# Five post- and pre-norms of a decoder layer: the sum of squares by one product with ones on all partitions, root and Newton step on full rows instead of a diagonal spread

## The chip, the cores and the metric

The kernel runs on one core of one Trainium2 chip. The metric is the device time of one execution in microseconds (us), as the median of three runs. The engines are named as in the profile: PE (TensorE, the matmul array), PEld (its weight loads), DVE (VectorE), ACT (ScalarE), POOL (GpSimd) and SP (which issues most transfers).

## The reference

One layer of a hybrid decoder trunk runs for a prompt of 512 tokens and for 32 sample tokens (8 sequences of 4). All is float32. Cut to what matters here:

```python
def _rmsnorm(x, g):
    x32 = x.astype(jnp.float32)
    y = x32 * lax.rsqrt(jnp.mean(x32 * x32, axis=-1, keepdims=True) + EPS) * g
    return y

def _layer(x, ...):
    m, ... = _mixer(_rmsnorm(x, norm_mix_pre), ...)      # projections, LRU branch, attention branch, w_out
    x = x + _rmsnorm(m, norm_mix_post)
    f, ... = _conv_ffn(_rmsnorm(x, norm_ffn_pre), ...)   # w_up (1024 x 8192), conv, gelu gate, w_down (4096 x 1024)
    x = x + _rmsnorm(f, norm_ffn_post)
```

`x` is 544 tokens by 1024 features. A norm needs, for every token, the sum of squares over 1024 features, the reciprocal root r of its mean, and the product of each feature with r and the feature's gain. The change touches the last three norms of the layer (`norm_mix_post`, `norm_ffn_pre`, and a part of `norm_ffn_post`), not the first.

## The kernel before, in words

Activations lie feature-major: a tile has 128 features on the partitions and tokens along the columns, so 1024 features are eight tiles. The 544 tokens are cut into two halves. Around the norms they are columns 0 to 272 and 272 to 544 (`HALF2`, 272 columns each); in the down projection they are 0 to 256 and 256 to 544 (`HALF`, so the second has 288). Every product is made in three parts: weights and activations are split into a high part (ACT) and the rest, the low part (DVE), and PE multiplies high by high, high by low and low by high.

**A norm, with features on the partitions.** ACT squares each of the eight tiles, DVE adds the squares up in one accumulator (`acc`, `accx`). The sum over the 128 partitions that remains is made by PE in `stats` (L1029): each block of 128 tokens of the accumulator is the stationary operand against one column of ones, so that the sums come out with tokens on the partitions, one column for each block (`pst`, 128 x 3 in PSUM). The last block has only 16 tokens of its own and is padded with zeros by a POOL memset. `newton_rstd` (L389) then makes r on these three columns: a square root on ACT, a scale, a reciprocal and a Newton step on DVE. As the tokens must come back along the columns, `diag` (L1041) scales the identity by r, block by block (`dg`), and `spread` (L1048) multiplies ones by that diagonal: `rep`, 128 x 272 in PSUM, holds r of each token on all partitions. Eight scalar_tensor_tensor instructions on DVE then take tile times gain times `rep`.

**Order of the work.** PE runs strictly as the code is written (manual schedule). Through the product with `w_out` ("out", L1229 copies its results into `mt`) ACT and DVE are ordered by the scheduler, which puts instructions written under `high_priority` ahead by 150 places; from `order_` on, behind the "out" product, ACT and DVE too run as the code is written. Work beside the main loop is written as generators: `start_at` registers one, and each `tick` (half a step of "out", or one slot of about twelve matmuls later) advances those whose time has come. A `yield 0.5` therefore means one slot later, `yield 1.0` two slots.

**Where the norms stand.** `norm_chain(a, acc)` (L1112) holds two norms for half a: `m` (`norm_mix_post`: sum, then `mt` times gain times r, x added by POOL or DVE, squares of the new x into `accx`) and `f` (`norm_ffn_pre`: sum, then `x1` times gain times r into `h2f` or `h2t`, then its high and low parts `b11`, `b21` for the first half, `b12`, `b22` for the second, which the first up products read). In each: `stats` in one slot, `diag` in the next (`YS`), `spread` and the use in the one after (`YA`, `YB`). The chain of half 0 runs while PE makes "out" for half 1; the chain of half 1 runs while PE makes the early up products (`pq`, L1396) of half 0, four pairs of column blocks by two halves of the features, sixteen units of twelve matmuls. In each slot `consumed` splits the weights of a unit four slots ahead (`wh_e` on ACT, `wl_e` on DVE). Behind the sixteen units PE transposes some state rows (`psf`) and then begins the same products for half 1.

At the end, `finish_b` (L1654) does the last norm for the second half's 288 columns: its sum is `stats` over `acc` and over `sq7` (the squares of the last tile, kept apart), then `diag`; two slots later come `spread` and the eight `ft` products with POOL additions. Between them stand held-back down products for half 0, whose results DVE adds into `ft`; then PE transposes `ft` (`turned`, tile `pfo`) and makes the last two blocks of 128 tokens with tokens on the partitions (`tokens`, `ends`), whose own norm (`ssq`, `rstd`) the change does not touch.

All working tiles of 128 x 572 come from one pool of ten (`T`, `T_BUFS`).

Of the kernel before, what the change touches and what calls it, by code (L numbers as in the profile page):

```python
# [14 lines left out]
ALU = mybir.AluOpType  # L15
AX = mybir.AxisListType

P = 128
# [105 lines left out]
def hawk_step(ctx, tc, I, O):  # L124
# [21 lines left out]
    def T(name, dt=F32):  # L146
        return tp.tile([P, FLAT + 4], dt, tag="t", name=name)
# [10 lines left out]
    def SM(name, shape, tag="sm"):  # L158
        return smp.tile(shape, F32, tag=tag, name=name)
# [4 lines left out]
    def mm(out, l, r, start, stop):  # L164
        pe.matmul(out, l, r, start=start, stop=stop)  # L165
# [223 lines left out]
    def newton_rstd(r, v, s_, sq):  # L389

        act.activation(s_, sq, AF.Sqrt, scale=1.0 / D, bias=epst)
        dve.tensor_scalar(v, sq, 1.0 / D, EPS, ALU.mult, ALU.add)
        dve.reciprocal(r, s_)
        mul(s_, r, r)
        stt(s_, s_, -0.5, v, ALU.mult, ALU.mult)
        stt(r, s_, 1.5, r, ALU.add, ALU.mult)
# [629 lines left out]
    mixer.close()  # L1026


    def stats(acc, nch, nm, more=None):  # L1029

        ps = PX("pst_" + nm)
        for z in range(nch):
            mm(ps[:, z:z + 1], acc[:, z * P:(z + 1) * P], ones[:, 0:1], z == 0, more is None and z == nch - 1)
        for z in range(nch if more is not None else 0):
            mm(ps[:, z:z + 1], more[:, z * P:(z + 1) * P], ones[:, 0:1], False, z == nch - 1)
        st = SM("nst_" + nm, [P, 3, 4], "nst")
        v, r, s_ = (st[:, z, :nch] for z in range(3))
        newton_rstd(r, v, s_, ps[:, :nch])
        return r

    def diag(r, n, nm):  # L1041
        dg = T("dg_" + nm)
        for z in range((n + P - 1) // P):
            w = min(P, n - z * P)
            dve.tensor_scalar(dg[:, z * P:z * P + w], ident[:, :w], r[:, z:z + 1], None, ALU.mult)
        return dg

    def spread(dg, n, nm):  # L1048

        rep = PX("rep_" + nm)  # L1050
        mm(rep[:, :n], ones, dg[:, :n], True, True)
        return rep

    def sq_sum(acc, src, n, first, nm):
        if first:
            act.activation(acc[:, :n], src, AF.Square)
            if n % P:
                pool.memset(acc[:, n:n + P - n % P], 0.0)
        else:
            sq = T("sq_" + nm)  # L1060
            act.activation(sq[:, :n], src, AF.Square)
            add(acc[:, :n], acc[:, :n], sq[:, :n])
# [49 lines left out]
    def norm_chain(a, acc):  # L1112
        lo, hi = HALF2[a]
        n = hi - lo
        nch = (n + P - 1) // P
        with tc.high_priority(offset=HP):
            r = stats(acc, nch, f"m{a}")
            yield YS[a]
            dg = diag(r, n, f"m{a}")
        yield YA[a]  # L1120
        with tc.high_priority(offset=HP):
            rep = spread(dg, n, f"m{a}")
            acc2 = T(f"accx{a}")
            sq = {}

            def x1_(c):
                return x1[c][:, lo:hi]

            for c in range(0 if a else 8):
                m_ = mt[c][:, lo:hi]  # L1130
                stt(m_, m_, pv[:, G_POST + c:G_POST + c + 1], rep[:, :n], ALU.mult, ALU.mult)
                pool.tensor_tensor(out=x1_(c), in0=x1_(c), in1=m_, op=ALU.add)
                sq_sum(acc2, x1_(c), n, c == 0, f"x{a}_{c}")
            for g in range(6 if a else 0):
                for c in range(2 * g, 2 * g + 2) if g < 4 else ():
                    m_ = mt[c][:, lo:hi]
                    stt(m_, m_, pv[:, G_POST + c:G_POST + c + 1], rep[:, :n], ALU.mult, ALU.mult)
                    if c % 2 == 0:
                        pool.tensor_tensor(out=x1_(c), in0=x1_(c), in1=m_, op=ALU.add)
                if g < 4:  # L1140
                    add(x1_(c), x1_(c), m_)
                for c in range(2 * g - 3, 2 * g - 1) if 1 <= g < 6 else ():
                    if 0 <= c < 8:
                        sq[c] = acc2 if c == 0 else T(f"sq_x{a}_{c}")
                        act.activation(sq[c][:, :n], x1_(c), AF.Square)
                        if c == 0 and n % P:
                            pool.memset(acc2[:, n:n + P - n % P], 0.0)
                for c in range(2 * g - 5, 2 * g - 3) if g < 5 else range(5, 8):
                    if c > 0:
                        add(acc2[:, :n], acc2[:, :n], sq[c][:, :n])  # L1150
                yield 0.5
        yield NORM_TICKS[a]
        with tc.high_priority(offset=HP):
            r = stats(acc2, nch, f"f{a}")
            yield YS[a]
            dg = diag(r, n, f"f{a}")
        yield YB[a]
        with tc.high_priority(offset=HP):
            rep = spread(dg, n, f"f{a}")

            def normed(c, dst):
                stt(dst, x1[c][:, lo:hi], pv[:, G_FPRE + c:G_FPRE + c + 1], rep[:, :n], ALU.mult, ALU.mult)

            def first(k2):
                return h2f[k2][:, 0:2 * HN]

            if a == 0:
                for k2 in range(5):
                    if k2 < 4:
                        for c in (2 * k2, 2 * k2 + 1):  # L1170
                            normed(c, h2_half0(c))
                        act.activation(operand2(("b11", "b21")[k2 // 2], k2 % 2, 0), first(k2), AF.Copy)
                    if k2:
                        o = [operand2(("b11", "b21")[(k2 - 1) // 2], (k2 - 1) % 2, j) for j in range(2)]
                        sub(o[1], first(k2 - 1), f32(o[0]))
                return
            n2 = {}

            def second(k2):
                return n2[k2]  # L1180

            def high(nm, src):
                for k in range(2):
                    act.activation(operand2(nm, k, 0), src(k), AF.Copy)

            def low(nm, src):
                for k in range(2):
                    sub(operand2(nm, k, 1), src(k), f32(operand2(nm, k, 0)))

            for k2 in range(5):  # L1190
                if k2 < 4:
                    n2[k2] = npool.tile([P, 2 * HN], F32, name=f"h2t{k2}")
                    for z in range(2):
                        normed(2 * k2 + z, n2[k2][:, z * HN:(z + 1) * HN])
                    act.activation(operand2(("b12", "b22")[k2 // 2], k2 % 2, 0), n2[k2], AF.Copy)
                if k2:
                    o = [operand2(("b12", "b22")[(k2 - 1) // 2], (k2 - 1) % 2, j) for j in range(2)]
                    sub(o[1], n2[k2 - 1], f32(o[0]))
                if k2 in (2, 4):
                    yield 0.5  # L1200
            for c in range(8):
                nc.sync.dma_start(out=x1d[c], in_=x1[c][:, 0:NT])
            t2 = [T(f"t2_{k}")[:, 0:2 * HN] for k in range(2)]
            for k in range(2):
                sub(first(k), first(k), second(k))
                stt(t2[k], first(k), -1.0, second(2 + k), ALU.mult, ALU.subtract)
                yield 0.5
            for k in range(2):
                add(first(2 + k), first(2 + k), t2[k])
                yield 0.5  # L1210
            high("t2", lambda k: t2[k])
            yield 0.5
            low("t2", lambda k: t2[k])
            yield 0.5
            for k in range(2):
                sub(second(k), second(k), second(2 + k))
                yield 0.5
            yield TX
            for nm, src in (("t3", second), ("t1", first), ("t4", lambda k: first(2 + k))):
                high(nm, src)  # L1220
                yield TY
                low(nm, src)
                yield TY
# [428 lines left out]
    sq7 = {}  # L1652

    def finish_b(acc):  # L1654

        lo, hi = HALF[1]
        n = hi - lo
        dg = diag(stats(acc, 3, "o1", sq7), n, "o1")
        yield FB[0]
        rep = spread(dg, n, "o1")  # L1660
        for c in range(8):
            f_ = ft[c][:, lo:hi]
            stt(f_, f_, pv[:, G_FPOST + c:G_FPOST + c + 1], rep[:, :n], ALU.mult, ALU.mult)
            pool.tensor_tensor(out=f_, in0=f_, in1=x1r[c][:, lo:hi], op=ALU.add)
            if c % 2:
                yield 0.5
# [178 lines left out]
```

## Time and profile before

| | us |
|---|---|
| median of three runs | 1009.07 (1008.91 to 1009.62) |
| the profiled execution, its own time | 1010.02 |
| its span, first to last instruction | 1008.1 |
| PE busy, with 7835 matmuls | 995.6 (99%) |
| DVE busy, 1553 instructions | 731.6 (73%) |
| ACT busy, 1422 instructions | 579.8 (58%) |
| POOL busy, 270 instructions | 151.5 (15%) |
| granted TensorE clock, mean | 0.995 |

By the chain of work that ended last and by the timeline, the first half's norms lie between 423 and 447 us, the second half's between 448 and 475, and the last norm between 982 and 992.

A row of the timeline reads: start, length, engine, line, operation, output <- inputs, shapes, count, and in brackets the idle time of the engine before it with what ended it. A group reads: line, engine, operation, count, then busy time and mean ns of one, then idle time and its releaser. A program sees float32 products of PE as two entries each, which is why three products show as x6.

### The profile page before, as it was taken

The page shows a single profiled execution, that of the slowest core. Times are in us where ns is not written, and L with a number is a line of the kernel's source. Part 1 is how long each engine was busy: PE and PEld are TensorE (multiplying, and loading weights), DVE is VectorE, ACT ScalarE, POOL GpSimd, SP SyncE. Part 2 cuts the span into 40 slices and gives each one's busy share as a digit, 9 for nine tenths or more (in the row PEclk, how much of TensorE's full clock was granted, in tenths as well). Part 3 has the DMA queues.
Part 4 walks back from the last instruction along what each step waited for, and adds up shares of the span by engine and source line. Part 5 has one row for each costly group of instructions (what it writes and reads, how often), then busy time and mean ns, then how long its engine had stood idle before and what let it go on. Part 6 is the DMA issues. An engine that isn't in the chain of part 4 may idle for free.

```text
span 1008.1 us, 20186 instructions
## 1 busy us (share of the span) xinstructions
PE 995.6 (99%) x7835; PEld 985.3 (98%) x7835; DVE 731.6 (73%) x1553; ACT 579.8 (58%) x1422; POOL 151.5 (15%) x270
## 2 busy tenths in 40 slices
PE   8999999999999999999999999999999999999997
PEld 7999999999999999999999999999999999999996
DVE  6476688444945655489787687878888888887865
ACT  6444554458448634556776656565656565656662
POOL 3131010001403432020000111111111111110004
PEclk9999999989999999999999999999999999999999
DMA  7743222322323245317235858585858676767712
GB/s 210 229 149 92 63 85 86 105 85 68 111 74 105 86 138 144 109 44 239 79 91 137 181 136 179 137 189 130 191 126 191 126 189 135 179 147 178 215 45 89
DMA packets 207687, 133.40 MB, mean 132 GB/s; under 512 B 6546, under 2 KB 194306, under 8 KB 207560
## 3 DMA queue, kind: packets, MB, share of 16 engines
q1 hardware_dynamic: 197944, 112.20, 39.2%
q0 software_dynamic: 9600, 17.90, 11.3%
q10 hardware_dynamic: 48, 2.03, 0.5%
q8 instruction: 61, 1.00, 0.4%
q14 instruction: 34, 0.28, 0.1%
HBM read 111.82 MB, written 9.14 MB: 120 GB/s over the span
## 4 chain that ended last, share of the span: by engine, by line
PE 93%; DVE 3%; DMA 2%; ACT 2%; issue 0%; SPq 0%; ACTq 0%; DVEq 0%
PE pmin L165 22%; PE pmdn L165 17%; PE pux L1396 15%; PE puy L1396 7%; PE pq L1396 6%; PE pmout L165 5%; PE pmao L165 5%; PE pmlo L165 4%; PE puz L1396 4%; PE pg L165 1%; PE psc L165 1%; PE pvp L165 1%; DMA raw_up_s<-in_w_up_dram 1%; DMA raw_in<-in_w_in_dram 1%; PE pt L701 1%; PE ptok L165 1%
## 5 line engine op out<-in xcount | busy, mean ns | idle before, releaser
L165 PE MATMUL pmin<-hH,wh_in 128*128 128x256 f32 (+1 forms) x576 | 168.0, 294 | 0.0
L165 PE MATMUL pmin<-hH,wl_in 128*128 128x256 f32 (+1 forms) x576 | 165.6, 290 | 0.0
L165 PE MATMUL pmin<-hL,wh_in 128*128 128x256 f32 (+1 forms) x576 | 165.5, 289 | 0.0
L165 PE MATMUL pmdn<-fH,wh_dn 128*128 128x256 f32 (+1 forms) x448 | 129.2, 288 | 0.2 <-DVE ft L174 0.2
L165 PE MATMUL pmdn<-fH,wl_dn 128*128 128x256 f32 (+1 forms) x448 | 129.2, 288 | 0.2 <-DVE wl_dn L168 0.2
L165 PE MATMUL pmdn<-fL,wh_dn 128*128 128x256 f32 (+1 forms) x448 | 129.1, 288 | 0.0
L177 DVE SCALAR_TENSOR_TENSOR uc<-u,fv,uc 128x560 f32<-128x560 f32 x128 | 102.0, 797 | 13.3 <-ACT uc L1427 13.2
L165 PEld LDWEIGHTS pmin<-hH,wh_in 128*128 128x128 f32 x576 | 109.2, 190 | 1.7 <-issue 0.6
L165 PEld LDWEIGHTS pmin<-hL,wh_in 128*128 128x128 f32 x576 | 109.2, 191 | 0.0
L165 PEld LDWEIGHTS pmin<-hH,wl_in 128*128 128x128 f32 x576 | 108.8, 190 | 0.0
L165 PEld LDWEIGHTS pmdn<-fH,wh_dn 128*128 128x128 f32 x448 | 84.3, 188 | 0.6 <-issue 0.6
L165 PEld LDWEIGHTS pmdn<-fH,wl_dn 128*128 128x128 f32 x448 | 84.4, 188 | 0.4 <-DVE wl_dn L168 0.4
L165 PEld LDWEIGHTS pmdn<-fL,wh_dn 128*128 128x128 f32 x448 | 84.3, 188 | 0.0
L1522 ACT COPY u<-pux 128x272 f32<-128x272 f32 x52 | 20.1, 386 | 85.4 <-PE pux L1396 85.3
L168 DVE TENSOR_TENSOR u<-puy,u 128x240 f32<-128x240 f32 (+2 forms) x78 | 24.6, 344 | 49.8 <-PE puy L1396 32.5
L174 DVE TENSOR_TENSOR ft<-ft,pmdn 128x256 f32<-128x256 f32 (+1 forms) x104 | 45.2, 435 | 16.6 <-PE pmdn L165 16.0
L277 ACT ACTIVATE wh_in<-raw_in 128x512 fp32r<-128x512 f32 x72 | 44.2, 628 | 20.8 <-PE pmin L165 10.4
L282 DVE TENSOR_TENSOR wl_in<-raw_in,wh_in 128x512 fp32r<-128x512 f32 x72 | 48.2, 683 | 1.6 <-ACT wh_in L277 1.5
L1427 ACT ACTIVATE uc<-u,fv 128x560 f32<-128x560 f32 x64 | 48.2, 755 | 0.0
L664 ACT ACTIVATE s<-s,st 128x256 f32<-128x256 f32 (+1 forms) x32 | 15.2, 476 | 50.7 <-DVE st L661 43.3
L168 DVE TENSOR_TENSOR wl_dn<-raw_dn,wh_dn 128x512 fp32r<-128x512 f32 x56 | 38.3, 685 | 0.0
L1322 POOL DMA_DIRECT2D raw_up_s<-raw_up_s x26 | 22.7, 872 | 101.7 <-issue 5.2
(773 smaller groups left out, 3415.7 us busy)
## 6 DMA issues: line engine op xcount, KB each, us to landing
raw_in<-in_w_in_dram SPq DMA_DIRECT2D x36, 512.0 KB
raw_dn<-in_w_down_dram SPq DMA_DIRECT2D x56, 256.0 KB
raw_up_s<-in_w_up_dram SPq DMA_DIRECT2D x26, 512.0 KB
raw_up_s<-raw_up_s POOLq DMA_DIRECT2D x26, 256.0 KB, 6.1
raw_ao<-in_w_attn_o_dram SPq DMA_DIRECT2D x8, 512.0 KB
raw_lo<-in_w_lru_o_dram SPq DMA_DIRECT2D x8, 512.0 KB
raw_out<-in_w_out_dram SPq DMA_DIRECT2D x8, 512.0 KB
x1d<-x SPq DMA_DIRECT2D x8, 272.0 KB
```

Of the source, the lines that this page charges most:

```text
L165: pe.matmul(out, l, r, start=start, stop=stop)
L168: dve.tensor_tensor(out=out, in0=a, in1=b, op=ALU.subtract)
L174: dve.tensor_tensor(out=out, in0=a, in1=b, op=ALU.add)
L177: dve.scalar_tensor_tensor(out=out, in0=a, scalar=s_, in1=b, op0=op0, op1=op1)
L277: act.activation(hl[0], raw, AF.Copy)
L282: (eng or dve).tensor_tensor(out=hl[1], in0=raw, in1=f32(hl[0]), op=ALU.subtract)
L664: act.activation(s3[:, j, :], s3[:, j, :], AF.Exp, bias=ng[:, j:j + 1], accum_out=sm[:, j:j + 1])
L701: pe.transpose(pt[:, (2 * ch + j) * P:(2 * ch + j + 1) * P], s3[:, j, ch * P:(ch + 1) * P], ident)
L1322: pool.dma_start(out=w["p4"], in_=w["p2"], accum_op=ALU.add)
L1396: pe.matmul(ps[:, :HN], w, x, start=start and k == 0 and i == 0, stop=stop and k == 3 and i == 2, skip_group_check=True)
L1427: act.activation(yt[j][:, 0:FLATU], u[:, 0:FLATU], AF.Copy, scale=fv[:, j:j + 1])
L1522: act.copy(e[nm_], z)
```

## The change

The sum over partitions is now one product with the whole 128 x 128 block of ones as the stationary operand and the accumulator as the moving one: every partition of the result holds the sum of every token, with tokens along the columns. Root and Newton step run on 128 x 272 (288 in the last norm) instead of 128 x 3, with the result and two working values in tiles of the pool `T`; the result stays in SBUF. `diag`, `spread` and the padding memsets are gone. Root and Newton step are written one `yield` later than before, where `diag` was (in `finish_b`: where `spread` was, two slots later).

```diff
-    def stats(acc, nch, nm, more=None):
+    def sums_(acc, n, nm, more=None):
 
         ps = PX("pst_" + nm)
-        for z in range(nch):
-            mm(ps[:, z:z + 1], acc[:, z * P:(z + 1) * P], ones[:, 0:1], z == 0, more is None and z == nch - 1)
-        for z in range(nch if more is not None else 0):
-            mm(ps[:, z:z + 1], more[:, z * P:(z + 1) * P], ones[:, 0:1], False, z == nch - 1)
-        st = SM("nst_" + nm, [P, 3, 4], "nst")
-        v, r, s_ = (st[:, z, :nch] for z in range(3))
-        newton_rstd(r, v, s_, ps[:, :nch])
+        mm(ps[:, :n], ones, acc[:, :n], True, more is None)
+        if more is not None:
+            mm(ps[:, :n], ones, more[:, :n], False, True)
+        return ps
+
+    def rstds(ps, n, nm):
+
+        r, v, s_ = (T(z + nm)[:, :n] for z in ("nr_", "nv_", "ns_"))
+        newton_rstd(r, v, s_, ps[:, :n])
         return r
-
-    def diag(r, n, nm):
-        dg = T("dg_" + nm)
-        for z in range((n + P - 1) // P):
-            w = min(P, n - z * P)
-            dve.tensor_scalar(dg[:, z * P:z * P + w], ident[:, :w], r[:, z:z + 1], None, ALU.mult)
-        return dg
-
-    def spread(dg, n, nm):
-
-        rep = PX("rep_" + nm)
-        mm(rep[:, :n], ones, dg[:, :n], True, True)
-        return rep
 
     def sq_sum(acc, src, n, first, nm):
         if first:
             act.activation(acc[:, :n], src, AF.Square)
-            if n % P:
-                pool.memset(acc[:, n:n + P - n % P], 0.0)
...
     def norm_chain(a, acc):
...
         with tc.high_priority(offset=HP):
-            r = stats(acc, nch, f"m{a}")
+            ps = sums_(acc, n, f"m{a}")
             yield YS[a]
-            dg = diag(r, n, f"m{a}")
+            rep = rstds(ps, n, f"m{a}")
         yield YA[a]
         with tc.high_priority(offset=HP):
-            rep = spread(dg, n, f"m{a}")
             acc2 = T(f"accx{a}")
...
                         act.activation(sq[c][:, :n], x1_(c), AF.Square)
-                        if c == 0 and n % P:
-                            pool.memset(acc2[:, n:n + P - n % P], 0.0)
...
         with tc.high_priority(offset=HP):
-            r = stats(acc2, nch, f"f{a}")
+            ps = sums_(acc2, n, f"f{a}")
             yield YS[a]
-            dg = diag(r, n, f"f{a}")
+            rep = rstds(ps, n, f"f{a}")
         yield YB[a]
         with tc.high_priority(offset=HP):
-            rep = spread(dg, n, f"f{a}")
...
     def finish_b(acc):
...
-        dg = diag(stats(acc, 3, "o1", sq7), n, "o1")
+        ps = sums_(acc, n, "o1", sq7)
         yield FB[0]
-        rep = spread(dg, n, "o1")
+        rep = rstds(ps, n, "o1")
```

More of the change, by code (lines that the diff above doesn't have):

```diff
@@ L1114, in norm_chain @@
         n = hi - lo
-        nch = (n + P - 1) // P
         with tc.high_priority(offset=HP):
-            r = stats(acc, nch, f"m{a}")
+            ps = sums_(acc, n, f"m{a}")
             yield YS[a]
-            dg = diag(r, n, f"m{a}")
+            rep = rstds(ps, n, f"m{a}")
         yield YA[a]
         with tc.high_priority(offset=HP):
-            rep = spread(dg, n, f"m{a}")
             acc2 = T(f"accx{a}")
```

## The prediction

> **What bounds the kernel now.** I read the page first (busy time, then the chain that ended last), then the same chain between 415 and 520 us where four of the five changed norms lie, then PE's waits there, then VectorE (DVE) in order of time.
>
> ```profile
> PE 995.6 (99%) x7835; PEld 985.3 (98%) x7835; DVE 731.6 (73%) x1553; ACT 579.8 (58%) x1422; POOL 151.5 (15%) x270
> PE 93%; DVE 3%; DMA 2%; ACT 2%; issue 0%; SPq 0%; ACTq 0%; DVEq 0%
> 447.00:475.00 28.00, 27.60 (x218) 27.04 (x217) 25.40 (x62) 15.09 (x35) 3.07 (x4) 1.00 0.62 194
> PE pst_f L165 <- DVE accx L174: 0.4, 1, 0.4
> ```
>
> TensorE (PE) is busy 99% of the span and carries 93% of the chain, at full granted clock (1.00 in the third row, whose columns are length, PE, weight loads, DVE, ACT, POOL, clock, DMA share, GB/s). So a microsecond of PE work removed is a microsecond won, if PE never has to wait longer than now. The third row is the warning: from 447 to 475 us, where the second half's two norms run, DVE is busy 25.4 of 28 us, and the one wait of PE in this stretch (fourth row) is for DVE's last addition into `accx`. There the kernel is a DVE chain with PE just behind it. That is where the change puts more DVE work.
>
> ```profile
> 423.23 0.56 PE pst_m L165 x6
> ...
> 437.87 0.56 PE pst_f L165 x6
> ...
> 446.53 1.51 PE pq L1396 x12
> 448.05 0.80 PE pst_m L165 x6
> ...
> 464.87 0.83 PE pst_f L165 x6
> ...
> 473.79 0.87 PE psf L1384 x8
> 474.66 42.16 PE pq L1396 x336
> ```
>
> These are pieces of the chain (start, length, what). A norm costs PE a `pst` (six entries for three one-column products) and later a `rep`, one product of 272 columns (two entries).
>
> **PE: work removed.** The new sum is one product of the shape of `rep`, and `rep` itself goes. So the saving per norm is the `pst`: 0.56 + 0.56 + 0.80 + 0.83 = 2.75 us in four norms. At the end of the kernel the `pst` has twice the entries:
>
> ```profile
> 982.33 1.23 PE pst_o L165 x12
> 986.53 0.48 PE rep_o L165 x2
> ```
>
> There 1.71 becomes two products of 0.48, 0.75 saved. Altogether 3.5 us of PE, if nothing stalls. The POOL memsets of the padding go too; nothing waits on POOL for them, so nothing for that.
>
> **DVE: work added.** Now the order on DVE round the second half's first norm:
>
> ```profile
> 447.82 1.35 DVE L168 TENSOR_TENSOR b21L<-h2f,b21H 128x544 fp32r<-128x544 f32 x2
> 449.18 0.16 DVE L392 TENSOR_SCALAR nst_m<-pst_m 128x3 f32<-128x3 f32 x1
> 449.26 0.17 DVE L393 RECIPROCAL nst_m<-nst_m 128x3 f32<-128x3 f32 x1
> 449.46 0.16 DVE L171 TENSOR_TENSOR nst_m<-nst_m 128x3 f32<-128x3 f32 x1
> 449.66 0.36 DVE L177 SCALAR_TENSOR_TENSOR nst_m<-nst_m 128x3 f32<-128x3 f32 x2
> 449.93 0.69 DVE L168 TENSOR_TENSOR wl_e<-raw_up__5740,wh_e 128x512 fp32r<-128x512 f32 x1
> 450.54 0.62 DVE L1045 TENSOR_SCALAR dg_m<-ident,nst_m 128x128 f32<-128x128 f32 x3
> 451.07 0.68 DVE L168 TENSOR_TENSOR wl_e<-raw_up__5738,wh_e 128x512 fp32r<-128x512 f32 x1
> 452.47 0.91 DVE L177 SCALAR_TENSOR_TENSOR mt<-mt,pv,rep_m 128x272 f32<-128x272 f32 x2 [0.71 <-PE rep_m L165]
> ```
>
> Newton on three columns takes 0.75 (449.18 to 449.93), the diagonal 0.53 (450.54 to 451.07): 1.28 in all. The prices on 272 columns:
>
> ```profile
> L509 DVE RECIPROCAL lz<-lz x1: 204/204/204, 59.4 to 59.4; 128x8 f32<-128x8 f32 x1
> L670 DVE RECIPROCAL st<-st 128x2 f32<-128x2 f32 x16 | 2.7, 166 | 0.6
> L177 DVE SCALAR_TENSOR_TENSOR mt<-mt,pv,rep_m 128x272 f32<-128x272 f32 x16 | 7.2, 488 | 1.4 <-PE rep_m L165 1.4
> L171 DVE TENSOR_TENSOR gl<-gl,pmlo 128x272 f32<-128x272 f32 x16 | 6.9, 431 | 1.3 <-PE pmlo L165 1.1
> 420.27 0.40 ACT L1229 ACTIVATE mt<-pmout 128x272 f32<-128x272 f32 x1 [2.14 <-PE pmout L165]
> ```
>
> A product or scale from PSUM takes 0.43, a scalar_tensor_tensor 0.49, and each step that needs the one before starts some 0.04 after its end (0.20 from start to start for 0.16 of work). The root on ACT goes from a few columns to the 0.40 of an activation of 272 columns.
>
> The term that decides is the reciprocal. Three columns take 0.17 us, eight take 0.204: 7.6 ns a column, where the other operations gain only some 1 ns a column (0.43 for 272 against 0.16 for 3). From eight to 272 columns that is 0.204 + 264 x 0.0076 = 2.2 us, far from any row, so it has two ends: 0.45 if the eight-column row is no slope at all and the reciprocal streams like the others, 2.2 by the slope. I take 2.2, because both rows are of this very operation. [...]
>
> The new Newton is then 0.35 (the scale overlaps the next) + 2.25 + 0.47 + 0.53 + 0.49 = 4.1 us on DVE in place of 1.28, in five norms, nearly all of it in the dependent chain.
>
> **First half (418 to 447 us).**
>
> ```profile
> 427.40 1.73 DVE L177 SCALAR_TENSOR_TENSOR mt<-mt,pv,rep_m 128x272 f32<-128x272 f32 x4 [0.73 <-PE rep_m L165]
> 427.98 6.92 POOL L1132 TENSOR_TENSOR x<-x,mt 128x272 f32<-128x272 f32 x8 [20.47 <-DVE mt L177]
> 430.85 0.61 DVE L174 TENSOR_TENSOR accx<-accx,sq_x 128x272 f32<-128x272 f32 x1
> 436.08 0.43 DVE L174 TENSOR_TENSOR accx<-accx,sq_x 128x272 f32<-128x272 f32 x1
> 442.14 1.72 DVE L177 SCALAR_TENSOR_TENSOR h2f<-x,pv,rep_f 128x272 f32<-128x272 f32 x4 [0.72 <-PE rep_f L165]
> 445.58 0.72 DVE L168 TENSOR_TENSOR b11L<-h2f,b11H 128x544 fp32r<-128x544 f32 x1
> ```
>
> Sum at 423.2, plus 0.5 product, 0.5 root, 4.1 of Newton, less the 0.35 that runs beside the root, with part of a weight split between: the eight `mt` products start near 428.4, 1.0 late. The old path waited 0.7 for `rep`, which is why it is not more. Beside POOL's additions a DVE addition of two SBUF tensors takes 0.61, alone 0.43, while the `mt` products, whose third operand is in PSUM, stay at 0.49. The new root lies in SBUF, so those products should get the same 0.1 to 0.2 each: 0.6 more over this loop. [...] `accx` is complete at 436.5 now, so 438.1; PE, 0.6 early by the first saving, reaches the second sum at 437.3 and waits 0.8. The second Newton runs from there to 443.0 against 442.14. The second `b11L` comes near 447.1, about when PE's first `pq` wants it (a quarter to a half of the way through the piece at 446.53). So PE enters the second half about where it does now: the savings of two norms are eaten by waits, and DVE is 1.0 late.
>
> **Second half (447 to 477 us).** ACT and DVE now take work as it is written, and PE consumes a unit of weights every 1.5 us. The Newton steps move one slot back, behind one `wl_e`; behind them are queued the next `wl_e`, the `mt` products and all that follows. So b21L ends at 450.2 instead of 449.2, `wl_e` 450.8, Newton 454.9, `wl_e` 455.5, and the `mt` products start at 455.5 against 452.47: 3.0 late. The loop after it is full DVE up to the sum at 464.87, so nothing is made up; contention adds 0.2. PE waits for `accx` (and a little for the late `wl_e`) some 4 to 5 us, having nothing else in its order.
>
> ```profile
> 466.54 0.15 DVE L392 TENSOR_SCALAR nst_f<-pst_f 128x3 f32<-128x3 f32 x1
> 469.39 1.72 DVE L177 SCALAR_TENSOR_TENSOR h2t<-x,pv,rep_f 128x272 f32<-128x272 f32 x4 [0.89 <-issue]
> 473.93 1.54 DVE L168 TENSOR_TENSOR b22L<-h2t,b22H 128x544 fp32r<-128x544 f32 x2
> ```
>
> The last norm: now 2.85 from Newton's start to the `h2t` products (0.89 of it idle); then one `wl_e` and 4.1, 4.7 in all: 1.8 more. DVE is 5.0 late at the last `b22L`, 480.5 instead of 475.5. PE reads it first after one `pq` of 1.5 and half of another behind 474.66, that is at 476.9: 1.4 of slack. So PE comes out 3.6 late. Behind it the chain is one PE piece of 42 us; nothing gives it back.
>
> **The end.**
>
> ```profile
> 985.31 0.74 DVE L174 TENSOR_TENSOR ft<-ft,pmdn 128x256 f32<-128x256 f32 x2
> 987.05 0.94 DVE L177 SCALAR_TENSOR_TENSOR ft<-ft,pv,rep_o 128x288 f32<-128x288 f32 x2 [1.00 <-PE rep_o L165]
> 987.91 0.41 DVE L174 TENSOR_TENSOR ft<-ft,pmdn 128x256 f32<-128x256 f32 x1
> 989.80 0.44 PE pfo L1696 x4
> ```
>
> `finish_b` now takes root and Newton only after its pause, where `rep` stood. They follow the two `ft` additions, which end near 985.3 since PE is a little earlier; 288 columns need 4.2 us, so the `ft` products start at 989.5 instead of 987.05, and the `ft` addition behind the first two (987.91) ends at 990.8. PE's `pfo` transposes need that one: they would come at 989.0, by 0.75 saved, and go at 990.9, 1.1 later than the 989.80 of now. ACT's copy of `pfo` stands behind a square that waits for DVE's `frow`, itself behind four more products: 2 us late. The rest of the end is a serial chain: 1.7 late, between 1.1 and 2.0.
>
> **Sum.** 3.6 + 1.7 = 5.3 us slower. The profiled execution took 1010.02 (span 1008.1 and 1.9 round it), which gives 1015.3; it stands 0.95 above the median of the runs, 1009.07, so on that scale 1014.4.
>
> **Rivals.** First, the reciprocal streams at 0.45 and the new chain is 2.3 us. Then each norm's result is ready at or before the old `rep` (0.7 to 0.9 of idle was spent waiting for it), DVE is 1.1 ahead in the second half, PE keeps 1.8 to 2 of its 2.75, and 0.4 at the end: 1006.8, faster. The point from which it decides is a Newton of about 2.9 us, a reciprocal of 1.0. For it: the eight-column row is one single instruction; against it: at two and three columns the same operation takes 0.17 in every row, so it does not scatter by 0.04.
>
> Second, the price is right but half of the lateness is swallowed: the first half absorbs its own, the split of weights runs ahead, and the end's ACT chain hides 1 us. Then some 1.5 + 0.5 of loss against the forecast's 5.3 would be left, at 1010.5. Against it: DVE has 0.7 and 0.9 of idle in the second half, and I have already spent both.
>
> Third, a place that I have not priced: three working tiles of 272 columns come from the ten shared temporaries, where one diagonal did. If a square or a `u` tile has to wait for one of them, a step of 4 us repeats once: 1018.5. For it: they are held through a reciprocal; against it: no wait of the page now names a temporary.
>
> **How the numbers follow.** Forecast 0.72, fast reciprocal 0.10, absorbed 0.08, temporaries 0.10. With the reciprocal between 1.9 (the slope from two to eight columns) and 2.2, contention nothing to 1 us and the end's two bounds, the forecast itself reaches from 1011.5 to 1017. The range is 1010.5 to 1019, which leaves out the first rival and a part of the others. A measurement of this kernel can tell 0.2%, 2.0 us, from no change: faster 0.09, same 0.09, slower 0.82.
>
> **What would show it.** Right: a RECIPROCAL of 272 columns near 2.2 us; PE idle before the sum near 465 of several us on `accx`, and a shorter one at the first products of the second half; DVE busy some 14 us more; PE's busy time about 3.5 less; `pfo` waiting on DVE. Wrong: a reciprocal under 1 us, or PE waits in 417 to 480 that add up to less than the 2.75 saved.

## The result, and the profile after

The changed kernel takes 1026.29 us (median of five runs, 1024.76 to 1027.73), the kernel before in the same runs 1008.91 (1005.94 to 1009.62): ratio 1.0177, 95% interval 1.0163 to 1.0191. So it is 17.4 us slower, where 5.3 were forecast and the range ended at 1019. The profiled execution is the one of 1024.76, span 1022.9.

The page of the kernel after, busy times and the engines' shares of the chain that ended last:

```profile
PE 993.8 (97%) x7801; PEld 981.8 (96%) x7801; DVE 748.4 (73%) x1538; ACT 580.7 (57%) x1422; POOL 152.0 (15%) x264
PE 84%; DVE 9%; ACT 3%; DMA 2%; issue 2%; SPq 0%; POOL 0%; ACTq 0%; DVEq 0%; POOLq 0%
```

The window of the second half's norms, with the columns explained in the prediction:

```profile
447.00:475.00 28.00, 23.89 (x167) 22.51 (x166) 26.71 (x51) 14.25 (x32) 3.59 (x4) 0.94 0.47 154
```

PE's waits from 400 us on (total us, times, longest), without the two shortest:

```profile
PE pst_f L165 <- DVE accx L174: 5.8, 2, 4.5
PE pux L1378 <- DVE wl_s_p L168: 2.8, 1, 2.8
PE pyo L1655 <- ACT yo L1657: 2.3, 1, 2.3
PE pq L1378 <- DVE b11L L168: 1.2, 2, 0.8
PE pfo L1678 <- DVE ft L174: 1.0, 1, 1.0
PE pq L1378 <- ACT b11H L1154: 1.0, 1, 1.0
PE pq L1378 <- DVE wl_q L168: 0.8, 1, 0.8
PE pq L1378 <- DVE wl_e L168: 0.7, 1, 0.7
PE pq L1378 <- DVE b22L L168: 0.4, 1, 0.4
```

Before, PE carried 93% of the chain and waited 0.4 us at one sum; now it carries 84%, and nine rows of waits stand there, 16 us together. The clock column of the window has fallen from 1.00 to 0.94, so PE lost speed too, not only time.

To see where the time went, take the starts of the same PE instructions in both traces, counted from the first sum (423.07 us before, 420.06 after). What lies ahead of that sum is the same work; the profiled run of before lost 2.9 us there to a drop of the granted clock between 200 and 224 us (0.86), which that of after did not have (1.00). All stages below are differences of such starts.

| stage | before | after | change |
|---|---|---|---|
| first sum to second (first half, `m` to `f`) | 14.64 | 18.59 | +3.95 |
| second to third (first half `f`, to the second half's `m`) | 10.34 | 14.48 | +4.14 |
| third to fourth (second half, `m` to `f`) | 16.82 | 19.01 | +2.19 |
| fourth to `psf` | 8.76 | 8.10 | -0.66 |
| `psf` to the last norm's sum | 508.53 | 513.54 | +5.01 |
| from there to the end of the span | 25.94 | 29.12 | +3.18 |

The sum is 17.81. The first half has lost 8.1, where the forecast had none; the second half 1.5 up to `psf`; the long stretch of up and down products behind it 5.0; the end 3.2. The 5.0 have two parts. Instruction by instruction, 1.8 of them are lost by 533 us: PE waits 0.43 for `b22L`, the last product of the second half's norm, and 0.78 for `wl_q`, a weight split of DVE, both in the list above. The other 3.2 are lost at one place, the wait of 2.77 for `wl_s_p` near 944 and the slow products behind it.

VectorE (DVE) in the first half of the kernel after, in order of time:

```profile
422.29 1.84 DVE L393 RECIPROCAL nr_m<-ns_m 128x272 f32<-128x272 f32 x1
424.05 0.63 DVE L168 TENSOR_TENSOR wl_e<-raw_up__5725,wh_e 128x512 fp32r<-128x512 f32 x1
424.59 0.43 DVE L171 TENSOR_TENSOR ns_m<-nr_m 128x272 f32<-128x272 f32 x1
424.94 0.69 DVE L168 TENSOR_TENSOR wl_e<-raw_up__5727,wh_e 128x512 fp32r<-128x512 f32 x1
...
427.20 3.69 DVE L177 SCALAR_TENSOR_TENSOR mt<-mt,pv,nr_m 128x272 f32<-128x272 f32 x5
430.82 1.02 DVE L174 TENSOR_TENSOR accx<-accx,sq_x 128x272 f32<-128x272 f32 x1
431.75 1.01 DVE L177 SCALAR_TENSOR_TENSOR mt<-mt,pv,nr_m 128x272 f32<-128x272 f32 x1
...
443.32 0.44 DVE L174 TENSOR_TENSOR acc<-acc,sq_wo 128x272 f32<-128x272 f32 x1 [4.37 <-ACT sq_wo L1048]
443.70 0.44 DVE L392 TENSOR_SCALAR nv_f<-pst_f 128x272 f32<-128x272 f32 x1
444.06 1.84 DVE L393 RECIPROCAL nr_f<-ns_f 128x272 f32<-128x272 f32 x1
```

POOL beside the `mt` products, and ACT ahead of the second Newton step, in the same view:

```profile
427.84 4.63 POOL L1117 TENSOR_TENSOR x<-x,mt 128x272 f32<-128x272 f32 x5 [32.04 <-DVE mt L177]
...
442.43 0.40 ACT L1211 ACTIVATE mt<-pmout 128x272 f32<-128x272 f32 x1 [4.30 <-PE pmout L165]
```

Four things are to be read here. The reciprocal takes 1.84 us, less than was feared. The steps of the first Newton do not follow each other: three weight splits (`wl_e`, two of them shown) and an addition into `acc` stand between them and the `mt` products, 2.1 us together, so that these products start 7.1 us after their sum began (427.20 and 420.06), where they started 4.3 after it before (427.40 and 423.07). An `mt` product beside POOL's additions takes 1.0 us instead of 0.48. And the second Newton step, whose sum PE began at 438.65, starts only at 443.70: DVE stands in the addition `acc<-acc,sq_wo`, which waits for ACT's square, which waits for ACT's copy, which waits for an "out" product that PE makes after the sum.

PE in order of time at that sum, after:

```profile
438.65 1.27 PE L165 MATMUL pst_f<-accx,ones 128*128 128x272 f32 x2 [4.47 <-DVE accx L174]
440.40 0.43 PE L165 MATMUL pmout<-mH,wh_out 128*128 128x272 f32 x1
440.63 0.43 PE L165 MATMUL pmout<-mL,wh_out 128*128 128x272 f32 x1
```

The window of these rows; the third number from the end is the granted clock:

```profile
438.00:442.00 4.00, 3.35 (x13) 3.12 (x14) 0.94 (x3) 0.13 (x1) 0.00 (x0) 0.57 0.02 6
```

After 4.47 us of waiting PE runs at a clock of 0.57: products 0.23 us apart that are 0.125 apart elsewhere, until 442. Shorter waits had a slow clock behind them too: after PE's three waits for `b11H` and `b11L` between 449 and 452 us (0.97, 0.38 and 0.80) the granted clock is 0.50 from 453 to 455, and after the 2.77 near 944 it is 0.50 from 944 to 946.

### The profile page after: what moved, and what is told of

It is laid out like the page before. It is cut to its first block, busy times and chain, and to the rows that moved or that the text cites. A ratio compares the mean times of both kernels' runs of the same rounds, so it can differ in the third digit from the quotient of the medians.

```text
span 1022.9 us, 20102 instructions
## 1 busy us (share of the span) xinstructions
PE 993.8 (97%) x7801; PEld 981.8 (96%) x7801; DVE 748.4 (73%) x1538; ACT 580.7 (57%) x1422; POOL 152.0 (15%) x264
## 4 chain that ended last, share of the span: by engine, by line
PE 84%; DVE 9%; ACT 3%; DMA 2%; issue 2%; SPq 0%; POOL 0%; ACTq 0%; DVEq 0%; POOLq 0%
PE pmin L165 21%; PE pmdn L165 16%; PE pux L1378 15%; PE puy L1378 7%; PE pmao L165 5%; PE pmlo L165 4%; PE puz L1378 4%; PE pmout L165 3%; DVE uc L177 2%; PE pq L1378 2%; PE pg L165 1%; PE psc L165 1%; PE pvp L165 1%; DMA raw_up_s<-in_w_up_dram 1%; ACT uc L1409 1%
## 5 line engine op out<-in xcount | busy, mean ns | idle before, releaser
L165 PE MATMUL pmout<-mH,wh_out 128*128 128x272 f32 x128 | 37.9, 296 | 0.0
```

## The experiments

**1. factor_in_psum.** The last Newton step writes into a PSUM tile.

```diff
-        stt(r, s_, 1.5, r, ALU.add, ALU.mult)
+        stt(out, s_, 1.5, r, ALU.add, ALU.mult)     # out = PX("rep_" + nm)[:, :n]
```

> The changed kernel, but the last Newton instruction of each norm writes the factor into PSUM, where the old spread product had it. Theory 'port': beside POOL's additions the products that read the factor from SBUF take 0.9 to 1.0 us each in the first half's loop and 0.8 at the end, against 0.49 and 0.51 with the factor in PSUM; so they go back to 0.5, the first half's second sum waits about 4 us less, PE stays warm there, and the end gains 2: 7 to 9 us faster than the changed kernel (1026.3), near 1018. Rival 'reciprocal': the products were slow only because DVE was late, the 1.84 us reciprocals are what costs; then not more than 2 us are won.

1018.82 (1018.66 to 1019.60), before beside it 1008.34: ratio 1.0105 (1.0090 to 1.0120), 7.5 us less than the changed kernel. The group of the `mt` products between 415 and 480 us, in the changed kernel:

```profile
L177 DVE SCALAR_TENSOR_TENSOR mt<-mt,pv,nr_m 128x272 f32<-128x272 f32 x16 | 10.3, 684 | 0.0
```

The same group in this run:

```profile
L177 DVE SCALAR_TENSOR_TENSOR mt<-mt,pv,rep_m 128x272 f32<-128x272 f32 x16 | 7.2, 488 | 0.0
```

With the factor in PSUM all sixteen products are back at 488 ns, among the same additions of POOL, and PE's longest wait at a sum falls from 4.5 to 2.2. By stages this takes 2.3 off the first, 1.0 off the second, 1.7 off the end (27.39), where the `ft` products go from 814 to 511 ns; from the first sum to the end it is 6.1 in all. So the place of the factor is a cause of its own.

How POOL slows these products can be read row by row in the changed kernel:

```profile
432.91 0.84 POOL L1117 TENSOR_TENSOR x<-x,mt 128x272 f32<-128x272 f32 x1 [0.44 <-DVE mt L177]
433.04 1.01 DVE L177 SCALAR_TENSOR_TENSOR mt<-mt,pv,nr_m 128x272 f32<-128x272 f32 x1
```

The product ends 0.30 after POOL's addition (434.05 and 433.75). So do all seven DVE instructions with two SBUF tensors of 272 columns that began during one of POOL's additions between 428 and 436 us. The kernel before has such rows too. Its addition of 0.61 at 430.85 began late in one of POOL's and ended 0.30 after it (431.45 and 431.15); this one began early and ended 0.30 after it as well (435.20 and 434.90):

```profile
434.18 1.02 DVE L174 TENSOR_TENSOR acc<-acc,sq_wo 128x272 f32<-128x272 f32 x1
```

**2. same_slot.** Root and Newton step are written in the slot of their sum, one `yield` earlier (two at the end).

```diff
             ps = sums_(acc, n, f"m{a}")
-            yield YS[a]
             rep = rstds(ps, n, f"m{a}")
+            yield YS[a]
```

> The changed kernel, but root and Newton are written in the slot of the sum (where the old three-column Newton stood), not one slot later (two at the end). Theory 'place': the first half's second Newton no longer stands behind an addition into acc that waits 4.4 us for PE, so it starts within 1 us of its sum instead of 4 to 5 after it, and the b11 waits of PE (2.2 us) go; at the end Newton starts 2.4 us earlier and pfo does not wait: 5 to 7 us faster, near 1020. Rival 'port and reciprocal': the order moves little because DVE is full anyway; then 0 to 2 us.

1022.44 (1020.58 to 1023.32), ratio 1.0137 (1.0120 to 1.0154): 3.9 less. DVE begins the second Newton step 1.8 us after its sum began, not 5.1:

```profile
440.13 0.44 DVE L392 TENSOR_SCALAR nv_f<-pst_f 128x272 f32<-128x272 f32 x1 [0.99 <-ACT ns_f L391]
```

The first stage falls by 0.7, the second by 2.1, the end by 0.7. That is less than the 5 to 7 us expected, and in the trace the stage from the fourth sum to `psf` grows by 2.7: behind two waits of PE (1.42 and 1.28) its products stand 0.23 us apart from 470 to 474, 0.125 between the two. From the first sum to the end the trace is only 1.7 shorter.

**3. psum_and_slot.** Both edits.

> Both of the above. If port and place are separate costs the gains add up: 12 to 15 us, near 1012, and what is left over the kernel before (1008) is the length of the Newton chain with its reciprocal less the PE work saved. If they are one cost seen twice (both only keep PE from waiting before the same two products), the sum is near the larger of the two, 1017 to 1018.

1016.48 (1015.66 to 1018.05), ratio 1.0078 (1.0061 to 1.0095): 9.8 less. That is under the 12 to 15 expected and lies between the larger of the two gains (7.5) and their sum (11.4); from the first sum to the end of the traces it is 7.1 less, beside 6.1 and 1.7. So most of each gain stays when the other is there, and the two are largely separate costs. The first two stages are left with +1.00 and +0.71 of their 8.1; PE still waits 2.4 us near 939 for `wl_s_p`.

**4. no_reciprocal.** The reciprocal is replaced by a scale with an offset, one pass; the factor is then not the reciprocal root.

```diff
-        dve.reciprocal(r, s_)
+        dve.tensor_scalar(r, s_, -0.5, 1.5, ALU.mult, ALU.add)
```

> The changed kernel with the reciprocal of the five norms replaced by a scale and offset of the same 272 columns (0.4 us instead of 1.84); the factor is then not the reciprocal root. Theory 'reciprocal': 1.4 us less on the chain at each of five places, 5 to 8 us faster with the clock that is kept, near 1019. Rivals 'port' and 'place': the first half's loop and its badly placed Newton stay, so that only 3 to 4 us are won (second half and end).

1016.11 (1014.58 to 1018.79), ratio 1.0080 (1.0059 to 1.0100): 10.2 less, for five reciprocals of 1.84 to 1.94 us that become passes of under 0.45 (the smallest group of DVE that is listed between 415 and 480 us has 0.44): by these rows an estimated 7 to 9.3 together. The `mt` products still take 687 ns, so contention is not what went; the first two stages fall by 2.2 and 3.3. More came back than was taken from DVE. Read from the trace, not tried by itself: PE's wait at the first half's second sum falls from 4.47 to 2.31, and no slow products follow it (0.125 us apart from 437.4 to 442). Runs 1, 2 and 4 shorten the same waits, so their gains overlap (7.5, 3.9 and 10.2 are together more than the 17.4, though all three keep the late weight).

**5. pad_start: the late weight near 940.** All four runs kept PE's wait for `wl_s_p`, though the orders of DVE and ACT in that stretch are those of before. DVE's row, after:

```profile
941.53 0.69 DVE L174 TENSOR_TENSOR p<-raw_up_s,raw_up__12547 128x512 f32<-128x512 f32 x1 [5.15 <-DMA raw_up_s<-in_w_up_dram]
```

The DMA queues of after while that load was under way, 933.2 to 941.5 us (packets, MB, share of sixteen engines):

```profile
q1 hardware_dynamic: 3054, 1.52, 70.2%
q0 software_dynamic: 144, 0.26, 17.2%
q8 instruction: 1, 0.02, 0.9%
```

DVE's row of before:

```profile
930.56 0.69 DVE L174 TENSOR_TENSOR p<-raw_up_s,raw_up__12575 128x512 f32<-128x512 f32 x1 [2.50 <-DMA raw_up_s<-in_w_up_dram]
```

The DMA queues of before, 923.6 to 930.6 us:

```profile
q1 hardware_dynamic: 2735, 1.36, 75.3%
q0 software_dynamic: 144, 0.26, 20.6%
```

Queue 8, of the kind "instruction", brings a piece about every 16 us, 61 pieces of 16 KB in the span. That these are PE's program is the author's reading: 1.00 MB over PE's 15.6 thousand products and weight loads comes to 64 bytes each. In before none falls into this load or the one a block earlier (890.6 to 896.8); in after one falls into each (at 901.2 and 933.5, and a third at 915.3 at the start of the load between). Its time, 0.9% of sixteen engines over 8.3 us, is 1.2 us of one engine. If that is a coincidence of phase (the new norms have fewer PE instructions, so the pieces end elsewhere), adding instructions where PE waits anyway should move it.

```diff
+    for z in range(20):
+        mm(pw[0:8, 0:8], ident[:, 0:8], ones[:, 0:8], True, True)
```

> The changed kernel with 20 more products of 8 by 8 at its start, where PE waits for the first rows anyway; the norms are those of the change. In the traces PE's program comes over DMA queue 8, one fetch of 16 KB about every 16 us, and in the changed kernel and the four variants so far a fetch falls into the loads of raw_up_s near 900 and near 933 us, in the kernel before into neither. The 80 added instructions bring each later fetch about 5 us earlier. Theory A, the late weight near 940 comes of those fetches: PE's wait of 2.8 us on wl_s_p goes, the clock there stays at 1.00, and the time falls from 1026.3 by 4 to 5 us, to about 1021.5. Theory B, the late weight comes of the order or the load of the vector engine after the new norms: the wait stays and the time is within 1 us of 1026.3.

1020.65 (1018.76 to 1022.25), before beside it 1007.70: ratio 1.0119 (1.0098 to 1.0140), 5.6 less with the norms untouched. PE's wait for `wl_s_p` is gone. DVE's row in this run:

```profile
939.67 0.70 DVE L174 TENSOR_TENSOR p<-raw_up_s,raw_up__12567 128x512 f32<-128x512 f32 x1 [2.04 <-DMA raw_up_s<-in_w_up_dram]
```

Its DMA queues, 932.4 to 939.7 us:

```profile
q1 hardware_dynamic: 3167, 1.58, 85.3%
q0 software_dynamic: 144, 0.26, 19.6%
```

DVE waits 2.0 for the load instead of 5.15, no piece of queue 8 lies in it or in the one a block earlier (900.2 to 906.6), PE does not wait, and the stage `psf` to the last sum shrinks from +5.01 to +1.32. Theory A holds for the late weight: about 3.7 of the 5.0 go when the pieces no longer fall into the loads. The 1.3 that are left are the waits for `b22L` (0.43) and `wl_q` (0.80), which the padding does not touch. From the first sum to the end the trace is 3.7 shorter; the rest of the 5.6 lies in the scatter of the times (3.5 us over the four runs).

**6. before_pad.** The counter-test: 38 such products at the start of the kernel before.

> The kernel before, its norms untouched, with 38 more products of 8 by 8 at its start. The 152 added instructions bring each later fetch of PE's program about 10 us earlier, into the loads of raw_up_s near 892 and near 929 us, where the kernel before has none. Theory A: PE waits 2 to 3 us on wl_s_p near 930 to 935, its clock dips there, and the kernel before becomes 3 to 5 us slower, about 1012, without any change of a norm. Theory B: 1008.3, or up to 1.5 us above it if the added products are not quite covered at the start, and no wait near 930.

1008.32 (1006.84 to 1009.52), ratio 0.9999 (0.9989 to 1.0008): no loss, against theory A's 3 to 5. DVE's row in this run:

```profile
928.51 0.69 DVE L174 TENSOR_TENSOR p<-raw_up_s,raw_up__12613 128x512 f32<-128x512 f32 x1 [3.62 <-DMA raw_up_s<-in_w_up_dram]
```

PE's longest wait between 900 and 960 us:

```profile
PE pux L1398 <- DVE wl_s_p L168: 1.3, 1, 1.3
```

Queue 8 during the second load, 920.8 to 928.5 us:

```profile
q8 instruction: 1, 0.02, 0.8%
```

The forecast of theory A failed here. The piece is in the second load, DVE waits 3.62 instead of 2.50, PE 1.3 instead of 0.1; the stage `psf` to the last sum is 1.1 longer. But no slow products stand behind PE's wait (0.125 us apart from 931.2 on), and the times do not show the 1.1: their interval ends at +0.8. So in this trace the load with a piece in it went with about 1 us more. In the changed kernel, where the late weight cost 3.2, pieces lay in the loads ahead of it as well (901.2 and 915.3), PE waited 2.8 us, and the clock was low behind that (0.87 from 940 to 945, 0.79 from 945 to 950). That these make up the difference is read from the two traces, not tried by itself.

**7. warm.** Eighteen products on PE just ahead of the first half's second sum.

> The changed kernel with 18 products of ones with the unit matrix on PE just ahead of the first half's second sum, where PE idles for 4.5 us. If the lower clock after that wait costs what the windows show (the sum 1.27 instead of 0.6 us, some ten products 0.1 us apart longer), 1.3 to 2 us go. The 72 added instructions also bring the later fetches 4.6 us earlier, so by theory A the wait near 940 goes as well and the sum is 5.5 to 7 us, about 1020; by theory B only the 1.3 to 2 us go, about 1024.5. If the clock costs nothing either, 1026.

1020.94 (1018.70 to 1022.31), ratio 1.0126 (1.0108 to 1.0144): 5.3 less, no more than the padding alone. The trace says more: no wait near 940 (these products are PE instructions added ahead of it too), the clock at the sum is 1.00, and the second stage is 12.54 against 14.47 in run 5. PE's row of the sum:

```profile
438.02 0.73 PE L165 MATMUL pst_f<-accx,ones 128*128 128x272 f32 x2 [0.44 <-DVE accx L174]
```

The window there:

```profile
438.00:442.00 4.00, 3.98 (x30) 3.90 (x31) 1.14 (x4) 1.21 (x3) 0.00 (x0) 1.00 0.01 2
```

So the cold clock was worth 1.9 us at this sum. Of these, 1.4 are lost again before `psf` (that stage is 9.49 against 8.06 in run 5), where after waits of 1.42 and 1.28 the products stand 0.23 us apart from 470.6 to 472.2. The four timed runs of each scatter over 3.5 us and do not show the difference.

**8. only_end.** The new norm at the end alone.

> The kernel before with the new norm at the end alone (288 columns); the four norms of the two halves are the old ones. By the aligned traces the end lost 2.9 us of the 17.4: about 1011.2. By the prediction's step for the end, 1.7 us: about 1010.0. By theory A and B alike no wait near 930, since all before the end is as it was. If the losses of the end exist only because PE arrives there late and cold, within 0.5 us of 1008.3.

1013.21 (1011.68 to 1014.06), ratio 1.0050 (1.0035 to 1.0065): 3.5 to 6.5 us lost by the interval, 3.5 by the trace (29.47 from the last sum to the end, against 25.94). All stages ahead are those of before to 0.1. The end needs none of the rest to lose its time, and loses about twice the 1.7 forecast. Its two longest waits of PE:

```profile
PE pyo L1689 <- ACT yo L1691: 2.3, 1, 2.3
PE pfo L1712 <- DVE ft L174: 1.0, 1, 1.0
```

**9. psum_slot_pad.** Runs 3 and 5 together.

> Factor in PSUM, root and Newton step in the slot of the sum, and the 20 small products at the start, together. By the two earlier runs alone (psum_and_slot 1016.5, the padded start worth 4 to 5.6 us) 1011 to 1012.5, with no wait on wl_s_p near 935. If the late weight there came of the fetch only as long as PE arrived late, the padding is worth nothing here: 1016.5.

1013.83 (1011.64 to 1016.34), before beside it 1007.12: ratio 1.0063 (1.0046 to 1.0079). By ratios that is 1.5 us under run 3, not the 4 to 5 expected; by the trace 4.7 (591.07 against 595.77 us from the first sum to the end). PE's wait for `wl_s_p` is gone, as expected. 2.7 of those 4.7 are a drop of the clock to 0.50 at 465 to 470 us in run 3 that the padded run, with the same PE waits up to there (1.28 twice), does not have; it waits 1.45 for `h2t` at 477 instead. How much the padding is worth here stays open between these two.

**10. one_lookup.** What the runs point to: the new sum in the two halves, then one lookup of ACT for the inverse root, a Newton step of four DVE passes that ends in PSUM, all in the slot of the sum; the old norm at the end; the padding at the start.

```diff
+        out, sq = PX("rep_" + nm)[:, :n], ps[:, :n]
+        act.activation(r, sq, AF.Abs_reciprocal_sqrt, scale=1.0 / D, bias=epst)
+        dve.tensor_scalar(v, sq, 1.0 / D, EPS, ALU.mult, ALU.add)
+        mul(s_, r, r)
+        stt(s_, s_, -0.5, v, ALU.mult, ALU.mult)
+        stt(out, s_, 1.5, r, ALU.add, ALU.mult)
```

> A version that could beat both: in the two halves the new sum, then the inverse root in one lookup of ACT (Abs_reciprocal_sqrt) in place of root and reciprocal, one Newton step on DVE with its last step into PSUM, all in the slot of the sum; at the end the old norm; 20 small products at the start. The reciprocal's 1.84 us and the 0.5 of contention per product leave the path in the halves, the 3.2 us of the end stay away, the late weight too, and the four norms keep PE's saved products. If these were the causes, the halves come out within 1 us of the kernel before and the time is 1006 to 1009. If the wide Newton step (three passes of some 0.45 us) still leaves more on the path than PE saves, 1010 to 1012.

1003.67 (1003.00 to 1004.34), ratio 0.9959 (0.9946 to 0.9973): 3.5 us faster than before, and better than was expected. The chain on its page:

```profile
PE 92%; DVE 3%; ACT 2%; DMA 2%; issue 1%; SPq 0%; ACTq 0%; DVEq 0%
```

The group of the lookups between 415 and 480 us:

```profile
L1068 ACT ACTIVATE nr_m<-pst_m,epst 128x272 f32<-128x272 f32 x2 | 1.0, 480 | 0.7 <-PE pst_m L165 0.7
```

PE's waits from 400 us on:

```profile
PE pst_f L165 <- DVE accx L174: 0.8, 1, 0.8
PE pmdn L165 <- ACT ffn_rows_s L1632: 0.4, 1, 0.4
PE pmdn L165 <- DVE ft L174: 0.2, 1, 0.2
```

PE carries 92% of the chain again. From the first sum to the end it needs 582.3 us against 585.0: 0.7, 0.8, 0.3 and 0.7 less in the first four stages, 0.3 in the long one, nothing at the end. The first four, 2.4 together, are near the 2.75 that the forecast gave to the removed PE products; they were there to be had, once DVE's chain was short. This run changes several things at once, and how much each gave is not shown; the padding alone gave the kernel before nothing (run 6, with 38 products).

## Why the prediction was wrong

The direction and the mechanism (a long Newton step on DVE, PE waiting behind it) were right, the size was not: 5.3 forecast, 17.4 measured. Point by point:

- **PE's saving** was right: each sum is one product of 0.6 us, and run 10 keeps 2.4 of the 2.75 in the four norms. In the changed kernel PE's busy time fell by 1.8, not 3.5, since products at a low clock count as busy longer: the first half's second sum took 1.27 us at a clock of 0.57, and 0.73 at 1.00 in run 7.
- **The reciprocal** was a little over-sized: 1.84 us for 272 columns, 1.94 for 288, 6.2 ns a column beyond the 0.204 for eight, against 2.2. It lay by the lower bound, 1.9, worked out from the slope between two and eight columns. That bound came from a row of the same operation, and held.
- **"The eight `mt` products start near 428.4, 1.0 late"** is the first step that failed. Against their sum they are 2.8 late. The reciprocal began 2.2 us after the sum, not 1.0, since ACT's root stood behind a copy and a square; and "part of a weight split", 0.45 in the sum, was three splits and an addition, 2.1. The reciprocal and the steps behind it, shorter than forecast, gave only 0.9 of this back. This is read from the trace; no run tries it alone.
- **"0.1 to 0.2 each, 0.6 more over this loop"** is the second. It took the size of the contention from one addition that began late in one of POOL's (0.61 against 0.43); the addition of 1.02 at 434.18 in the same trace was left out. Where POOL adds throughout, a product with both tensors in SBUF took 0.99 to 1.01 us for 0.48 and ended 0.30 after the addition beside it. That is 0.5 each, and run 1 puts 2.3 us on this loop and 1.7 on the end, where the same products had been costed at no contention at all.
- **"PE enters the second half about where it does now"** is the third. It let the second Newton step start as soon as its sum was made. On DVE the step stood behind an addition that waited for PE's own later product, 5.1 us after the sum began. Run 2 gives 2.1 us of the second stage and 0.7 of the first to that place. Forecast for the first half: nothing; measured: 8.1.
- **PE's wait "0.8" at the second sum** was 4.5, and it was not paid by its length alone: 1.9 us more were lost behind it at the low clock (14.47 for the second stage in run 5, 12.54 in run 7).
- **The second half's 3.6** was 1.5 up to `psf`, and 3.3 with the 1.8 that were lost behind it by 533 us. The total is near, but not by its parts, so that is luck: PE waits 1.3 at the sum, not the "several us" of the forecast, 0.66 for `wl_e` ahead of it, 0.43 for `b22L` and 0.78 for `wl_q` behind it, and a part of the loss is the clock of 0.50 from 453 to 455.
- **The end's 1.7** was 3.2 (3.5 in run 8). `pfo` waits on DVE 1.0 us, as forecast 1.1; what was missed is the products' 814 instead of 511 ns behind it.
- **"The chain is one PE piece of 42 us; nothing gives it back"** was incomplete. Nothing was given back, but 3.2 us more were lost near 940, where the change has no instruction. No step of the prediction looked at the transfers of queue 8.
- **The rivals.** The fast reciprocal (1006.8) and the absorbed lateness (1010.5) were both refuted. The temporaries (1018.5) gave a time nearest to the result by a cause that does not show: DVE's waits in the two halves end on `sq_wo`, `wh_e` and the root, none on a temporary.

By place the 17.8 us of the traces are 8.1 (first half) + 1.5 (second half up to `psf`) + 1.8 (behind it, by 533 us) + 3.2 (the late weight) + 3.2 (the end). By cause they do not divide cleanly, since the chain, the queue and the clock meet at the same waits.

## What to carry to other kernels

Price an elementwise operation by what runs beside it: moving one operand from PSUM to SBUF cost nothing where POOL was idle (493 and 499 ns) and doubled the time where POOL was adding (0.48 and 1.0 us). When a dependent chain of several microseconds replaces a short one, follow the order of work on its engine for what already waits there (5.1 us here), and count a PE wait of several microseconds together with the slow products that can follow it (4.5 and 1.9 us here). And before a loss far from an edit is explained by the edit, look whether the padding alone moves it.

## What the hardware showed that was not expected

- DMA queue 8 brings 61 pieces of 16 KB, one about every 16 us, while the weights are loaded; a piece inside the 512 KB load of `raw_up_s` went with 1.1 us more of DVE's wait (run 6, 3.62 for 2.50), and 20 tiny products at the start were worth 3.7 us to the changed kernel by the traces, 5.6 by the medians.
- A DVE product with two SBUF tensors beside POOL's additions did not slow by a share: it ended 0.30 us after the addition during which it began, so that it took 0.99 to 1.01 us for 0.48; with one of the tensors in PSUM it was undisturbed at 488 ns (run 1).
- The length of a PE wait alone did not tell whether a low clock follows. Behind a wait of 2.32 us near 940 in run 1 the products stood 0.23 us apart, behind one of 2.31 near 437 in run 4 0.125; three waits of 0.97, 0.38 and 0.80 close together in the changed kernel had a clock of 0.50 behind them, after one of 1.3 in run 6 the products stood 0.125 apart; and after the same two waits of 1.28 the clock from 465 to 470 us was 0.50 in run 3 and 1.00 in run 9.
